# Ranking of the experts moved behind the second expert's weight splits, the fixing of the ranked places' words moved into the second expert, and the first transposes made due later

## The chip, the cores and the metric

The kernel runs on one core of a Trainium2 chip, with everything it needs in the device's memory. The metric is the time of one execution on the device in microseconds, the median of several runs. The core has five engines with a queue each: TensorE (PE; its weight loads are listed as PEld), VectorE (DVE), ScalarE (ACT), GpSimd (POOL) and SyncE (SP). Each issues its instructions strictly in its queue's order, so one that waits holds up all that stand behind it. SyncE and GpSimd also issue most of the transfers between device memory and on-chip memory; 16 DMA engines carry them out.

## The reference

One decoder layer: a mixing part and a routed mixture of experts. The part that the change touches is the routing: each token takes the best of four groups, and the two best of its four experts.

```python
def hier_moe(x, w_rg, b_rg, w_re, b_re, w_gate, w_up, w_down):
    ...
    g_sel = jnp.argmax(g_logits, axis=-1)
    ...
    top_p, top_i = lax.top_k(e_prob, TOP_K_IN_GROUP)
    top_p = top_p / jnp.sum(top_p, axis=-1, keepdims=True)
    weights = p_g * top_p
    expert_id = g_sel[:, None] * EXPERTS_PER_GROUP + top_i
    combine = jnp.sum(jax.nn.one_hot(expert_id, N_EXPERTS, dtype=f32) * weights[..., None], axis=1)
    y = jnp.zeros(xf.shape, f32)
    for e in range(N_EXPERTS):
        h = jax.nn.silu(xt @ w_gate[e]) * (xt @ w_up[e])
        y = y + combine[:, e:e + 1] * (h @ w_down[e]).astype(f32)
    return y.reshape(B, L, D).astype(x.dtype)
```

There are 2048 tokens of width 1024 and 16 experts with a hidden width of 256. Ahead of this stand a projection, a pooling mixer, a gated linear attention and an output projection; behind it a final norm.

## The kernel before

The kernel has two large stages. The dense one runs over 16 tiles of 128 tokens: projections and attention first, then, tile by tile, the output projection (`out_proj`, three parts into the banks sp, o and ds) and the routing (`route_pick`, `route_rest`). For each tile, `route_rest` counts with small matmuls how many tokens each expert has so far, works out each token's slot, and writes a record of 32 bytes through an indirect transfer into the table in device memory. The second stage runs over the 16 experts, each with a fixed number of slots (up to 320, in row parts j of 128, 128 and 64). An expert's rows are gathered by the token numbers of its records (`gather`, `first_rows`), transposed on TensorE into the banks tp and zg (`transposes`, line 955), scaled and split by ScalarE (line 109, high part) and VectorE (line 110, low part), and multiplied by the expert's weights. All large products are made of three matmuls: high by high, low by high, high by low.

The weights come in chunks of 128 x 1024 numbers (512 KB), in the order of `stream`: four gate chunks and two down chunks for each expert. SyncE issues the loads (`load_chunks`, line 765) into five buffers (three called raw, two called wr); `split_chunk` splits each into a high part on ScalarE (line 113) and a low part on VectorE (line 114), which frees the buffer for a later chunk. The first ten chunks (both gates of the first two experts and the first one's down weights) belong to fixed experts. All later ones go by rank: the 14 other experts are worked on in the order of their token counts, so that the larger ones get the longer slots.

`rank_experts` finds that order on VectorE out of the final counts, and writes `place` (an expert's place) and `expert_at` (the expert at a place). SyncE reads `expert_at` place by place (`expert`, line 749) to address the loads: `load_places` (line 1115) loads the table words of the experts at each place into `tab`, and then `load_chunks` loads their weights. Each record also names the token's other expert, and `fix_words` (lines 1125 to 1131) works out from `place` which of the two is worked on second, and sets the words that the rows' stores and adding loads go by.

Two experts begin early: the rows that the first 13 tiles sent to the experts 0 and 1 are gathered while the last tiles are still routed (row parts 0 and 2), and `gate_rows` multiplies them ahead of the main loop; the rest (part 1) follows from `first_rows`. The first of these transposes were written with `added[0]`, so that they stand behind the last tile's first addition of the output projection. In the loop `between(i)` places work between the matmuls of an expert: transposes of the next expert, splits of coming chunks, the fixing of words.

A scheduler places each instruction in its engine's queue by priority and by the times that it assumes. Two helpers bind it: `must_follow` adds a wait, and `queued_after` only fixes the order within a queue.

## Time and profile before

| | before |
|---|---|
| median of 3 runs | 1103.26 us (1103.2 to 1103.97) |
| profiled execution | 1105.13 us, its span in the trace 1103.4 us |
| TensorE busy | 1048.4 us (95% of the span) |
| VectorE busy | 776.6 us (70%) |
| ScalarE busy | 562.8 us (51%) |
| GpSimd busy | 310.5 us (28%) |

Times in the trace are counted from the span's start. The dense stage ends at about 695 us, the early rows of the two fixed experts run from there to about 724 us, and the loop over the experts begins at about 733 us. A busy engine in these views is one that has an instruction under way; matmuls overlap, and the distance from one start to the next is what a matmul costs. In brackets behind a row stands how long the engine was idle before it and which instruction ended that by the profile; where the engine that is named had long been done, it was another, often a transfer.

### The profile page before, as it was taken

The numbers are of one execution on the slowest core, as the hardware profiler recorded it, in microseconds if no ns is written. First come the engines' busy times: TensorE is split into PE (matmuls) and PEld (weight loads), VectorE is DVE, ScalarE is ACT, GpSimd is POOL, SyncE is SP. The second block draws the span as 40 slices with busy tenths as digits, with TensorE's granted clock in tenths as the row PEclk, the third lists the DMA queues.
The fourth block names the chain that finished last, engine by engine and source line by source line (L and its number), as shares of the span: only waits on it lengthen the run. The fifth ranks groups of instructions, "written<-read, shape, count | busy, mean of one in ns | idle before, by whom it ended". The sixth has DMA issues, their size and how long they took to land. (4 is left out here: it accounts for less than half of the span.)

```text
span 1103.4 us, 19138 instructions
## 1 busy us (share of the span) xinstructions
PE 1048.4 (95%) x6614; PEld 940.3 (85%) x6614; DVE 776.6 (70%) x2674; ACT 562.8 (51%) x1192; POOL 310.5 (28%) x272
## 2 busy tenths in 40 slices
PE   6999999999999999999999999989999999998982
PEld 5888888888888889999999999668998989887961
DVE  6476666654555775887777788767777788887863
ACT  7544444434443552333333333557767777677731
POOL 2000000000000000110111013144777788876540
PEclk9999999999999999999999999999999999999996
DMA  8422232211112342444343345389888989899841
GB/s 289 162 67 77 93 112 93 68 49 58 52 66 84 115 158 101 163 135 137 124 148 133 114 145 194 113 230 303 210 246 228 260 248 239 232 281 330 219 152 61
DMA packets 63831, 173.43 MB, mean 157 GB/s; under 512 B 20532, under 2 KB 20837, under 8 KB 63728
## 3 DMA queue, kind: packets, MB, share of 16 engines
q1 hardware_dynamic: 36272, 105.72, 28.6%
q0 software_dynamic: 24864, 57.87, 19.9%
q10 hardware_dynamic: 2592, 8.55, 2.2%
q8 instruction: 54, 0.88, 0.3%
q14 instruction: 49, 0.40, 0.1%
HBM read 142.43 MB, written 56.43 MB: 180 GB/s over the span
## 5 line engine op out<-in xcount | busy, mean ns | idle before, releaser
L443 POOL DMA_DIRECT2D y_dram<-y x16 | 8.7, 541 | 390.6 <-DVE y L441 390.6
L689 POOL DMA_INDIRECT table<-rec,ix x32 | 32.8, 1026 | 190.3 <-DVE tmp L709 92.8
L933 POOL DMA_INDIRECT oe<-xr,tab x38 | 66.7, 1756 | 63.3 <-ACT xr L1061 46.2
L323 PE MATMUL mm<-wb,XL 128*128 128x512 f32 (+1 forms) x240 | 83.6, 349 | 0.0
L324 PE MATMUL mm<-wb,XH 128*128 128x512 f32 (+1 forms) x240 | 82.9, 345 | 0.0
L322 PE MATMUL mm<-wb,XH 128*128 128x512 f32 (+1 forms) x240 | 82.7, 344 | 0.0
L933 POOL DMA_INDIRECT xr<-oe,tab x37 | 73.3, 1981 | 17.6 <-issue 9.8
L525 PE MATMUL mm<-XL,ws 128*128 128x256 f32 (+1 forms) x256 | 73.1, 286 | 0.2 <-DVE XL L114 0.2
L524 PE MATMUL mm<-XH,ws 128*128 128x256 f32 (+1 forms) x256 | 73.1, 286 | 0.0
L526 PE MATMUL mm<-XH,ws 128*128 128x256 f32 (+1 forms) x256 | 72.3, 282 | 0.0
L113 ACT ACTIVATE XH<-xt 128x1024 fp32r<-128x1024 f32 x32 | 33.9, 1059 | 52.9 <-PE mm L526 32.8
L933 POOL DMA_INDIRECT out_dram<-xr,tab x37 | 51.4, 1388 | 22.1 <-DVE sr_y L62 9.3
L114 DVE TENSOR_TENSOR wb<-raw,wb 128x1024 fp32r<-128x1024 f32 x39 | 47.5, 1220 | 7.9 <-ACT wb L113 7.9
L985 PE MATMUL mm<-xl,ws 128*128 128x256 f32 (+2 forms) x168 | 51.3, 305 | 0.0
L984 PE MATMUL mm<-xh,ws 128*128 128x256 f32 (+2 forms) x168 | 51.0, 303 | 0.0
L986 PE MATMUL mm<-xh,ws 128*128 128x256 f32 (+2 forms) x168 | 50.9, 303 | 0.0
L322 PE MATMUL mm<-ws,XH 128*128 128x512 f32 x112 | 47.5, 424 | 2.0 <-ACT XH L113 2.0
L322 PEld LDWEIGHTS mm<-wb,XH 128*128 128x128 f32 x240 | 45.3, 189 | 4.6
L324 PEld LDWEIGHTS mm<-wb,XH 128*128 128x128 f32 x240 | 45.2, 188 | 4.7
L323 PEld LDWEIGHTS mm<-wb,XL 128*128 128x128 f32 x240 | 45.3, 189 | 4.3
L525 PEld LDWEIGHTS mm<-XL,ws 128*128 128x128 f32 x256 | 48.2, 188 | 0.7 <-DVE XL L114 0.4
L526 PEld LDWEIGHTS mm<-XH,ws 128*128 128x128 f32 x256 | 48.5, 189 | 0.3 <-issue 0.2
(663 smaller groups left out, 3842.5 us busy)
## 6 DMA issues: line engine op xcount, KB each, us to landing
raw<-in_wgu_e_dram SPq DMA_DIRECT2D x42, 512.0 KB, 5.7
xt<-in_xT_dram SPq DMA_DIRECT2D x32, 512.0 KB, 3.6
xn<-in_xn_dram SPq DMA_DIRECT2D x32, 512.0 KB, 3.5
wr<-in_wgu_e_dram SPq DMA_DIRECT2D x22, 512.0 KB, 6.2
raw<-in_wd_e_dram SPq DMA_DIRECT2D x20, 512.0 KB, 6.2
hn_dram<-xn ACTq DMA_DIRECT2D x16, 512.0 KB, 3.4
oe<-xn POOLq DMA_DIRECT2D x16, 512.0 KB, 4.2
wr<-in_wd_e_dram SPq DMA_DIRECT2D x12, 512.0 KB, 6.0
```

The source lines that it names most:

```text
L113: return (nc.scalar.activation(hi, src, AF.Copy), (eng or V).tensor_tensor(lo, src, hi.bitcast(F32), op=OP.subtract))
L114: (eng or V).tensor_tensor(lo, src, hi.bitcast(F32), op=OP.subtract))
L322: nc.tensor.matmul(q, xh[:, k, :], wh[:, c0:c1_], start=(k == 0), stop=False)
L323: nc.tensor.matmul(q, xl[:, k, :], wh[:, c0:c1_], start=False, stop=False)
L324: nc.tensor.matmul(q, xh[:, k, :], wl[:, c0:c1_], start=False, stop=(k == KB - 1))
L524: nc.tensor.matmul(ps[:, b], WS[k][0][:, c], XH[:, k, o:], start=(k == 0), stop=False)
L525: nc.tensor.matmul(ps[:, b], WS[k][0][:, c], XL[:, k, o:], start=False, stop=False)
L526: nc.tensor.matmul(ps[:, b], WS[k][1][:, c], XH[:, k, o:], start=False, stop=(k == KB - 1))
L933: return nc.gpsimd.indirect_dma_start(out=out_, out_offset=off if scatter else None, in_=in_, in_offset=None if scatter else off, bounds_c ...
L984: nc.tensor.matmul(p[:, c0:c1_], wh, xh, start=(k == 0), stop=False)
L985: nc.tensor.matmul(p[:, c0:c1_], wh, xl, start=False, stop=False)
L986: nc.tensor.matmul(p[:, c0:c1_], wl, xh, start=False, stop=(k == KB - 1))
```

## The change

Three things move. `rank_experts` no longer runs right behind the routing of the last tile, in the pool of work tiles of the dense stage, but inside the experts' stage, put in VectorE's queue behind the low part of the second expert's last gate chunk (`last_low`). It works in a tile `sq` that `fix_words` and others use as well, and the counts are kept in `place` itself. The two calls of `fix_words` for the ranked places, made in the loop of the second expert, are put in the queue behind the low part of the third expert's transposes that are written just ahead of them (`low[0]`). And the first transposes follow `added[1]` instead of `added[0]`.

```diff
@@ -172,8 +172,8 @@
     late1, late2, late3 = by_expert("late1", 1.0e9, 0.0), by_expert("late2", 0.0, 0.0), by_expert("late3", 0.0, 0.0)
     late_step2 = by_expert("late_step2", 16384.0, -16.0 - 6144.0)
     late0 = iota("late0", 16, 1, base=127 * 48 + 32, pool=sl)
-    counts = sl.tile([128, 16], F32, name="counts")
     place = per.tile([128, 16], F32, name="place")
+    counts = place
     expert_at = per.tile([128, 16], I32, name="expert_at")
     desc4 = iota("desc4", 4, -1, base=4, pool=sl)
     tok_all = iota("tok_all", NT, 128, pm=1)
@@ -711,25 +711,6 @@
         V.tensor_copy(sv[:, 6:7], r)
         return last
 
-    def rank_experts():
-
-        n = NE - FIXED
-        key = wk.tile([128, 16], F32, name="v16")
-        V.scalar_tensor_tensor(key, counts, 16.0, iota16, op0=OP.mult, op1=OP.subtract)
-        sq = wk.tile([128, 512], F32, name="sq", bufs=1)
-        g = sq[:, :n * n].rearrange("p (a b) -> p a b", a=n)
-        inner = lambda x: x[:, None, FIXED:].to_broadcast([128, n, n])
-        outer = lambda x: x[:, FIXED:, None].to_broadcast([128, n, n])
-        V.tensor_tensor(g, inner(key), outer(key), op=OP.is_gt)
-        V.tensor_copy(place[:, :FIXED], iota16[:, :FIXED])
-        V.tensor_reduce(place[:, FIXED:], g, axis=AX.X, op=OP.add)
-        V.tensor_scalar(place[:, FIXED:], place[:, FIXED:], float(FIXED), None, op0=OP.add)
-        V.tensor_tensor(g, inner(place), outer(iota16), op=OP.is_equal)
-        V.tensor_tensor(g, g, inner(iota16), op=OP.mult)
-        at = wk.tile([128, 16], F32, name="t1")
-        V.tensor_reduce(at[:, FIXED:], g, axis=AX.X, op=OP.add)
-        V.tensor_copy(expert_at[:, FIXED:], at[:, FIXED:])
-
 
     DW = [[WB[4 + f][h][:, :1024] for h in range(2)] for f in range(2)]
     stream = [("g", e, k) for e in range(2) for k in range(4)] + [("d", 0, f) for f in range(2)]
@@ -868,7 +849,6 @@
             route_rest(t - 1)
         route_pick(t)
     routed = route_rest(NT)
-    rank_experts()
     c1.close()
 
     rank = per.tile([128, NT], F32, name="rank")
@@ -920,7 +900,7 @@
               + [(xh1[:, k, :], xl1[:, k, :]) for k in range(2)]]
         HB = me.tile([128, 2, 2 * CAP], F32R, name="HB")
         tab_e = me.tile([128, 2, 2, 8], I32, name="tab_e")
-        hidden_done = [None]
+        hidden_done, low = [None], [None]
...
@@ -958,7 +938,7 @@
                     must_follow(t_, [after])
             c0, c1_ = min(cols[j] for j in js), max(cols[j] + rows[j] for j in js)
             xh, xl = XE[e % 2][k]
-            split_scaled(xh[:, c0:c1_], xl[:, c0:c1_], p[:, c0:c1_], nf[:, k:k + 1])
+            low[0] = split_scaled(xh[:, c0:c1_], xl[:, c0:c1_], p[:, c0:c1_], nf[:, k:k + 1])[1]
 
         def split_hidden(hb, h, c0, c1_):
 
@@ -1114,7 +1094,7 @@
         def load_places(lo, hi, which):
             must_follow(nc.sync.dma_start(by_place[:, :, lo:hi], table_by[:, :, which]), table_ops)
 
-        def fix_words(lo, hi, at):
+        def fix_words(lo, hi, at, after=None):
 
             n = hi - lo
             w = tabf.rearrange("p (j e) w -> p j e w", e=NE)[:, :, lo:hi]
@@ -1122,13 +1102,32 @@
             eq = sq[:, :3 * n * NE].rearrange("p (j e x) -> p j e x", j=3, e=n)
             second = sq[:, 384:384 + 3 * n].rearrange("p (j e) -> p j e", j=3)
             full = [128, 3, n, NE]
-            V.tensor_tensor(eq, w[:, :, :, 5:6].to_broadcast(full), iota16[:, None, None, :].to_broadcast(full), op=OP.is_equal)
+            o_ = V.tensor_tensor(eq, w[:, :, :, 5:6].to_broadcast(full), iota16[:, None, None, :].to_broadcast(full), op=OP.is_equal)
+            if after:
+                queued_after(o_, after)
             V.tensor_tensor(eq, eq, at[:, None, None, :].to_broadcast(full), op=OP.mult)
             V.tensor_reduce(second, eq, axis=AX.X, op=OP.add)
             V.tensor_tensor(second, second, iota16[:, None, lo:hi].to_broadcast([128, 3, n]), op=OP.is_lt)
             V.scalar_tensor_tensor(by_place[:, :, lo:hi, 2], second, -OOB, w[:, :, :, 6], op0=OP.mult, op1=OP.add)
             V.tensor_scalar(second, second, OOB, -OOB, op0=OP.mult, op1=OP.add)
             V.tensor_tensor(by_place[:, :, lo:hi, 1], second, w[:, :, :, 6], op=OP.add)
+
+        def rank_experts(after):
+
+            n = NE - FIXED
+            sq = mk.tile([128, D // 2], F32, name="sq")
+            g, key, at = sq[:, :n * n].rearrange("p (a b) -> p a b", a=n), sq[:, 200:216], sq[:, 216:232]
+            queued_after(V.scalar_tensor_tensor(key, counts, 16.0, iota16, op0=OP.mult, op1=OP.subtract), after)
+            inner = lambda x: x[:, None, FIXED:].to_broadcast([128, n, n])
+            outer = lambda x: x[:, FIXED:, None].to_broadcast([128, n, n])
+            V.tensor_tensor(g, inner(key), outer(key), op=OP.is_gt)
+            V.tensor_copy(place[:, :FIXED], iota16[:, :FIXED])
+            V.tensor_reduce(place[:, FIXED:], g, axis=AX.X, op=OP.add)
+            V.tensor_scalar(place[:, FIXED:], place[:, FIXED:], float(FIXED), None, op0=OP.add)
+            V.tensor_tensor(g, inner(place), outer(iota16), op=OP.is_equal)
+            V.tensor_tensor(g, g, inner(iota16), op=OP.mult)
+            V.tensor_reduce(at[:, FIXED:], g, axis=AX.X, op=OP.add)
+            V.tensor_copy(expert_at[:, FIXED:], at[:, FIXED:])
 
         table_rows = table.rearrange("(p n) w -> p n w", n=48)
         s_ = nc.gpsimd.dma_start(tab_e, table_rows.rearrange("p (j e) w -> p j e w", e=NE)[:, 0:2, 0:2])
@@ -1143,12 +1142,14 @@
             XG[e][1] = row_tile()
         with tc.high_priority():
             for k in range(KB):
-                transposes(0, k, (0, 2), added[0])
+                transposes(0, k, (0, 2), added[1])
         early = [gate_rows(0, 0, "mm"), gate_rows(0, 2, "mm", lambda k: k < 6 or transposes(1, k - 6, (0, 2)))]
         must_follow(picked[0], [gate_ops[6]])
         for k in range(4):
-            must_follow(split_chunk()[1], [routed])
+            last_low = split_chunk()[1]
+            must_follow(last_low, [routed])
             load_chunks(min(8 + k, 10))
+        rank_experts(last_low)
         for k in range(2, KB):
             transposes(1, k, (0, 2))
         load_places(0, FIXED, slice(0, FIXED))
@@ -1182,7 +1183,7 @@
                     for k in range(i, i + 2):
                         transposes(e + 1, k, None if e else (1,))
                 if e == 1 and i in (2, 6):
-                    fix_words(*((2, 9) if i == 2 else (9, 16)), place)
+                    fix_words(*((2, 9) if i == 2 else (9, 16)), place, low[0])
                 if e == 0:
                     if i == 0:
                         for op in load_chunks(10 + WRB, mk):
```

What the order of the queues makes of it, at three places. In the new kernel the lines of the helpers behind `rank_experts` have other numbers: the transposes are line 935, the fixing 1105 to 1113, the ranking 1120 to 1130; lines up to 711 keep theirs. Numbers behind an underscore tell buffers apart: wb_86 to wb_101 are the high and low halves of the second weight buffer (wb_86, wb_88, wb_90, wb_92 are the high parts of the second expert's gate chunks, wb_87 and so on the low ones; wb_94 to wb_97 are the down chunks; wb_98 to wb_101 hold rows of the second expert; in the dense stage all of them hold the output projection's weights), ws are the gate chunks of the first and third expert, and xh and xl those experts' transposed rows.

VectorE, the end of the ranking, before:

```order
L727 TENSOR_TENSOR sq<-place,iota_114 128x196
L709 SCALAR_TENSOR_TENSOR tmp,sv_all<-E,lev 128x16
L110 SCALAR_TENSOR_TENSOR wb_99<-zg,vecs,wb_98 128x192
L709 SCALAR_TENSOR_TENSOR tmp,sv_all<-E,lev 128x16
L728 TENSOR_TENSOR sq<-sq,iota_114 128x196
L114 TENSOR_TENSOR wb_87<-raw,wb_86 128x1024
L730 TENSOR_REDUCE t_8623<-sq 128x14
L114 TENSOR_TENSOR wb_89<-raw,wb_88 128x1024
L731 CAST expert_at<-t_8623 128x14
L114 TENSOR_TENSOR wb_91<-raw,wb_90 128x1024
```

and now:

```order
L114 TENSOR_TENSOR wb_97<-raw,wb_96 128x1024
L1126 TENSOR_SCALAR place<-place 128x14
L114 TENSOR_TENSOR HB<-zg,HB 128x2x128
L1127 TENSOR_TENSOR sq<-place,iota_114 128x196
L993 TENSOR_TENSOR h<-mm,h 64x256
L1128 TENSOR_TENSOR sq<-sq,iota_114 128x196
L1129 TENSOR_REDUCE sq<-sq 128x14
L114 TENSOR_TENSOR HB<-tp,HB 128x2x64
L1130 CAST expert_at<-sq 128x14
L110 SCALAR_TENSOR_TENSOR xl_8627<-zg,vecs,xh_8626 128x128
```

Before, the cast that writes `expert_at` stands between the low parts of the second and third gate chunk; now it stands behind the low parts of the first expert's down chunks (wb_95, wb_97) and behind the splits of the first expert's early hidden tiles (HB from zg and from tp).

VectorE, the first fixing instruction of the ranked places (line 1125, now 1105), before:

```order
L114 TENSOR_TENSOR HB<-tp,HB 128x2x64
L110 SCALAR_TENSOR_TENSOR xl_8640<-zg,vecs,xh_8639 128x128
L110 SCALAR_TENSOR_TENSOR xl_8640<-tp,vecs,xh_8639 128x128
L1125 TENSOR_TENSOR sq<-tab,iota_114 128x336
L110 SCALAR_TENSOR_TENSOR xl_8640<-zg,vecs,xh_8639 128x128
L1126 TENSOR_TENSOR sq<-sq,place 128x336
```

and now:

```order
L110 SCALAR_TENSOR_TENSOR xl_8627<-zg,vecs,xh_8626 128x320
L110 SCALAR_TENSOR_TENSOR xl_8627<-tp,vecs,xh_8626 128x320
L114 TENSOR_TENSOR ws_79<-raw,ws_78 128x1024
L110 SCALAR_TENSOR_TENSOR xl_8627<-zg,vecs,xh_8626 128x320
L1105 TENSOR_TENSOR sq<-tab,iota_114 128x336
L114 TENSOR_TENSOR wb_95<-wr,wb_94 128x1024
L1108 TENSOR_TENSOR sq<-sq,place 128x336
```

Before, it stands among the low parts of the first expert's late rows (128 columns); now it stands behind the low part of the third expert's first gate chunk (ws_79), among the low parts of the third expert's rows (320 columns).

TensorE, the first transposes, before:

```order
L572 MATMUL o<-wb_98,yh 128x348
L955 MATMUL tp<-ident,xs_8645 128x128
L955 MATMUL tp<-ident,xg 128x128
L955 MATMUL zg<-ident,xs_8645 128x128
L955 MATMUL zg<-ident,xg 128x128
L573 MATMUL o<-wb_98,yL 128x348
```

and now:

```order
L572 MATMUL ds<-wb_96,yh 128x348
L573 MATMUL ds<-wb_96,yL 128x348
L935 MATMUL tp<-ident,xs_8632 128x128
L935 MATMUL tp<-ident,xg 128x128
L935 MATMUL zg<-ident,xs_8632 128x128
L935 MATMUL zg<-ident,xg 128x128
L574 MATMUL ds<-wb_97,yh 128x348
```

Before, they stand in the second part of the last tile's output projection (bank o, behind its seventh matmul); now they stand in the third part (bank ds, behind its fifth matmul). The last of their eight rounds now ends behind the third part.

## Rows read from the trace of the kernel before

**Rows 1.** The page, first part: busy time of an engine, its share of the span, its instructions.

```profile
PE 1048.4 (95%) x6614; PEld 940.3 (85%) x6614; DVE 776.6 (70%) x2674; ACT 562.8 (51%) x1192; POOL 310.5 (28%) x272
```

**Rows 2.** Waits of TensorE, longest first in total: line that waited, line that it waited for, us in total, times, longest us. The first four are from the stretch 660 to 820 us, the last from 755 us to the end.

```profile
PE zg L955 <- DVE xl L110: 2.8, 1, 2.8
PE tp L955 <- DVE m L597: 1.5, 1, 1.5
PE zg L955 <- DVE wb L110: 1.2, 1, 1.2
PE sp L1006 <- DVE wb L114: 1.1, 1, 1.1
...
PE tp L955 <- ACT xr L1061: 7.1, 5, 3.0
```

**Rows 3.** TensorE in order of time, 684 to 762 us: start, duration, line, what it writes and reads, sizes, and in brackets the idle time before it.

```profile
685.07 0.33 PE L574 MATMUL o<-wb,yh 128*128 128x348 f32 x1
685.24 0.32 PE L572 MATMUL o<-wb,yh 128*128 128x348 f32 x1
687.04 0.30 PE L955 MATMUL tp<-ident,xs 128*128 128x128 f32 x1 [1.49 <-DVE m L597]
687.18 0.27 PE L955 MATMUL tp<-ident,xg 128*128 128x128 f32 x1
...
711.34 0.50 PE L1006 MATMUL sp<-wb,wb 128*128 128x512 f32 x1 [1.06 <-DVE wb L114]
...
712.37 0.63 PE L1004 MATMUL sp<-wb,wb 128*128 128x512 f32 x1
...
723.41 0.39 PE L1006 MATMUL o<-wb,xh 128*64 128x512 f32 x1
...
724.33 0.28 PE L955 MATMUL zg<-ident,xg 128*128 128x128 f32 x1
...
731.09 0.33 PE L955 MATMUL zg<-ident,xg 128*128 128x128 f32 x1 [2.77 <-DVE xl L110]
...
755.76 0.31 PE L986 MATMUL mm<-xh,ws 128*128 128x320 f32 x1
```

**Rows 4.** ScalarE in order of time: the high parts of the first and of the last gate chunk of the third expert.

```profile
742.78 1.06 ACT L113 ACTIVATE ws<-raw 128x1024 fp32r<-128x1024 f32 x1 [0.36 <-DVE HB L114]
...
751.93 1.07 ACT L113 ACTIVATE ws<-raw 128x1024 fp32r<-128x1024 f32 x1 [0.67 <-DMA raw<-in_wgu_e_dram]
```

**Rows 5.** VectorE in order of time, 706 to 755 us.

```profile
706.55 0.17 DVE L649 TENSOR_TENSOR counts<-m,counts 128x16 f32<-128x16 f32 x1
...
709.01 0.35 DVE L727 TENSOR_TENSOR sq<-place,iota 128x196 f32<-128x196 f32 x1
709.28 0.17 DVE L709 SCALAR_TENSOR_TENSOR tmp<-E,lev 128x16 f32<-128x16 f32 x1
...
709.37 0.41 DVE L110 SCALAR_TENSOR_TENSOR wb<-zg,vecs,wb 128x192 fp32r<-128x192 f32 x1
...
710.06 1.22 DVE L114 TENSOR_TENSOR wb<-raw,wb 128x1024 fp32r<-128x1024 f32 x1
...
712.60 0.17 DVE L731 CAST expert_at<-t 128x14 int32<-128x14 f32 x1
...
725.45 0.29 DVE L114 TENSOR_TENSOR HB<-tp,HB 128x128 fp32r<-128x128 f32 x1
...
730.27 0.51 DVE L1125 TENSOR_TENSOR sq<-tab,iota 128x336 f32<-128x336 f32 x1 [3.11 <-DMA tab<-table]
...
754.37 1.22 DVE L114 TENSOR_TENSOR ws<-raw,ws 128x1024 fp32r<-128x1024 f32 x1
```

**Rows 6.** SyncE: the reads of expert_at (durations in ns, least, median, most; first and last start in us), then its transfers in order of time (start, time from the first to the last issue's end, count).

```profile
L749 SPq TENSOR_LOAD <-expert_at x14: 262/270/727, 716.1 to 731.1; - x14
715.36 16.76 SPq L1115 DMA_DIRECT2D tab<-table  x15
...
733.02 0.35 SPq L765 DMA_DIRECT2D raw<-in_wgu_e_dram  x1
```

**Rows 7.** Transfers, by the stretch in which they were issued: line's tiles, queue, count, size, us from issue to landing. The first was issued between 733.0 and 733.1, the second between 745.0 and 745.5, the third between 680.2 and 681.0 us. Last, the part of GpSimd's queue in the stretch 740 to 744 us: packets, MB, share of the 16 engines' time.

```profile
raw<-in_wgu_e_dram SPq DMA_DIRECT2D x1, 512.0 KB, 5.4
...
raw<-in_wgu_e_dram SPq DMA_DIRECT2D x1, 512.0 KB, 6.8
...
xg<-hn_dram,tab_e POOLq DMA_INDIRECT x1, 4.3
...
q0 software_dynamic: 159, 0.59, 62.5%
```

**Rows 8.** Stretches: length, then busy us (instructions) of PE, PEld, DVE, ACT and POOL, TensorE's granted clock (1.00 is 2.4 GHz), mean busy share of the DMA engines, GB/s.

```profile
710.00:720.00 10.00, 8.94 (x37) 6.08 (x37) 8.40 (x16) 4.81 (x8) 2.68 (x3) 0.83 0.54 164
...
730.00:740.00 10.00, 8.91 (x43) 6.29 (x44) 8.54 (x28) 5.79 (x15) 4.15 (x3) 1.00 0.79 211
...
748.00:750.00 2.00, 2.00 (x14) 1.59 (x12) 2.00 (x3) 1.90 (x4) 0.00 (x0) 1.00 1.03 416
```

**Rows 9.** GpSimd in order of time: the last write of records into the table, the gather of the first expert's late rows, and a gather for the fourth expert.

```profile
710.53 1.61 POOL L689 DMA_INDIRECT table<-rec,ix  x1 [0.31 <-issue]
...
719.15 1.12 POOL L933 DMA_INDIRECT xg<-hn_dram,tab  x1 [7.01 <-DMA tab<-table]
...
740.15 1.04 POOL L933 DMA_INDIRECT xg<-hn_dram,tab  x1 [1.68 <-PE tp L955]
```

## The prediction

> **What bounds the kernel now.** I first read the shares of the engines: TensorE is busy for 95% of the span [rows 1], so only its few idle stretches and what they hide can matter. The second view is the list of its waits between 660 and 820 us, where the change works [rows 2]: four stalls of 2.8, 1.5, 1.2 and 1.1 us, 6.6 us in all. The third view puts them in order of time [rows 3]: 1.49 us ahead of 687.04 (the first transposes), the 1.2 and 1.1 us close together ahead of 711.34 (the rows of the second expert, behind the routing of the last token tile), 2.77 us ahead of 731.09. The reader should then see what else is late at the end of this stretch. At 751.93 ScalarE has waited 0.67 us for a weight load, and splits the last weights of the third expert [rows 4]; VectorE finishes their low part at 754.37 + 1.22 = 755.59 [rows 5], and TensorE takes it at 755.76 [rows 3]. So at 755 us the kernel is bound by weights that arrive just in time, not by TensorE's earlier stalls. After that its largest waits are a few for gathered rows, 7.1 us over 350 us [rows 2], so I take a shift at 755.76 to reach the end one for one.
>
> **Where those weights come from.** SyncE's queue issues in order: the table words of the first two experts at 715.36, then 14 times "read expert_at, load that expert's table words" (reads from 716.1 to 731.1), then the final norm's weights, then at 733.02 the first 512 KB chunk of the third expert [rows 6]. That chunk takes 5.4 us (to 738.4), and the sixth, issued just behind 745.0, lands 6.8 us later, at 751.9 [rows 7], which is the wait in rows 4. From 733.02 to 751.9 are 18.9 us.
>
> **The change, part by part.**
>
> First transposes due later. They now stand behind 22 more matmuls of the output projection, at 0.17 us each (685.07 to 685.24 [rows 3]): 685.4 + 3.7 = 689.1. The rows that they waited for were there at 687.04, so the 1.49 us go. Against it, the second pair of transposes needs a bank that VectorE frees only behind the routing instructions that the order puts ahead of it; following its queue I find it free some 0.4 us late. Net -1.1 us (bounds -1.5 and 0).
>
> Ranking out of the last routing. Between the counts at 706.55 and the first low split at 710.06 VectorE spends 3.5 us [rows 5]. Six ranking instructions lie in it: four of 196 elements at 0.27 us (709.01 to 709.28) and two small ones at 0.09 (709.28 to 709.37), so 1.26 us. The order puts two low parts of 192 columns there instead (0.41 each) and takes two small accumulations out (0.18): 3.5 - 1.26 + 0.82 - 0.18 = 2.9 us, 0.6 us less. TensorE's 711.34 becomes 711.34 - 1.1 - 0.6 = 709.6, or 710.0 if the low parts wait for their transposes, with four more transposes already done (0.14 us each, 687.04 to 687.18 [rows 3]): a lead of about 1.8 us. In before TensorE fell to its lower clock right after this stall: the matmul at 712.37 takes 0.63 us against 0.50 at 711.34 and 0.39 at 723.41 [rows 3], and the granted clock of 710 to 720 is 0.83 [rows 8], which is 0.17 of 10 us or 1.7 us lost. With a shorter stall it may stay at 2.4 GHz, 1.7 us more lead, or not.
>
> This lead does not last. The routing's own last cast comes only 0.3 us earlier (most of the ranking leaves ahead of it, three low parts enter). So the second table write (710.53 [rows 9]), the table words (715.36) and the gather of the first expert's late rows (719.15 [rows 9]) move by 0.3 us. That gather takes 4.3 us at the least (the quickest of its kind [rows 7]), 718.9 + 4.3 = 723.2, and TensorE needs its rows for the transpose that stands at 724.33 [rows 3]. It comes there at about 721 and waits about 2 us: the lead is 1.1 us at most.
>
> Fixing words in the second expert. At 730.27 VectorE has waited 3.11 us for the table words of the ranked places, with the low parts of the transposes queued behind it [rows 5], and TensorE stalls 2.77 us for that [rows 3]. In the new order these words come behind the third expert's low parts, some 15 us later, when they have long landed. The stall goes, and TensorE's lead grows to about 3.9 us. The fourteen fixing instructions, 0.5 us for the widest (730.27), then lie between the weight splits; one of the widest is ahead of the last split and costs 0.3 us there, where the split waits for ScalarE in part.
>
> Ranking behind the low parts. Here is the price. The cast that writes expert_at stood at 712.60 [rows 5], 3.5 us ahead of the first read at 716.1 [rows 6], so it cost nothing. In the new order it stands behind the split of the second early hidden tile (HB from tp). In before that split is at 725.45 [rows 5]; it needs TensorE's transposes of h, which stand one matmul ahead of the end of the second expert's 48 matmuls. Behind 710.0 these are 43 matmuls of 0.23 us (723.41 to 724.33 is four of them [rows 3]) and six transposes of 0.14, 10.7 us: 720.7. ScalarE's and VectorE's halves, the matmul and the cast are four short steps, 1.2 us: **the cast is at about 722.0** (721 if all goes well, 723.5 if the clock falls as in before). SyncE's queue stops there, with everything behind it. Its 14 reads and loads take as long as before, so the first chunk goes from 733.02 to 722.05 + (733.02 - 716.1) = 739.0, 6.0 us later.
>
> What of this hides. TensorE's lead hides nothing, since it ends in waiting for the weights themselves. Two things shorten the chain behind the first chunk. In before ScalarE came to it only at 742.78 [rows 4], 4.4 us after landing; now it waits for it, and the sixth chunk, whose buffer the first one's split frees, is asked for 7.8 us after the first instead of 12, which no longer binds. And the gathers of later experts, which shared the DMA engines with the chunks (0.59 MB on GpSimd's queue in 740 to 744, 62.5% of the engines' time [rows 7]), are now mostly ahead of 739. Bounds: with the same company the sixth chunk lands at 739.0 + 18.9 = 757.9, +6.0 us; with none, the five chunks behind the first follow it at 0.524 MB by the best rate near here, 416 GB/s [rows 8], 1.3 us each: 739.0 + 5.4 + 6.3 = 750.7, which is -1.2 us. I take the two gathers of 512 KB out of the company that fell behind the first chunk (the later one at 740.15 [rows 9]), 1.05 MB by 416 GB/s, 2.5 us: 755.4, +3.5 us. It is nearer the upper end because GpSimd still stores the first expert's rows in that stretch.
>
> The Trainium skill ("DMA: Bandwidth & Descriptors", Queues, rings and completion order) says that each DMA engine takes turns packet by packet between the queues that have work. By it the chunks have about half of the engines while GpSimd's queue has work and all of them otherwise, which would give the same two ends and leaves open only how long the company lasts; the 62.5% of rows 7 agree with a share of that kind.
>
> **The sum.** Sixth chunk +3.5, one fixing instruction +0.3: the low part at 755.59 and the matmul behind it come 3.8 us later. The leads of 1.1 and 2.8 us are spent in waiting for it. The profiled execution took 1105.13 us with a span of 1103.4; the median of the runs is 1103.26, and I add the shift to that: **1107.0 us**.
>
> **The rivals.**
> 1. The chunks catch up: GpSimd's queue is nearly empty after 739, chunks follow each other at 1.3 to 1.9 us, and the sixth lands before 753.8. Then the shift is -1 to +2 us, 1102 to 1105, which a measurement can't tell from no change (0.2%, 2.2 us). For it speaks that TensorE's lead moves the stores and gathers forward; against it, that the DMA engines were busy throughout in 748 to 750 (share 1.03 [rows 8]), 15 us behind the first chunk.
> 2. Faster: the lead of 3.9 us reaches the experts, 1099.4 us. It decides from the point at which the sixth chunk lands by 748, that is, if the cast comes by 714 or so, or the chunks are not held behind it. For it speaks the size of the removed stalls, most of 6.6 us. The order of the queues speaks against it.
> 3. A second price: TensorE now waits in pieces between 747 and 759 for each chunk, and the clock falls behind them, as after 711.34. That cost 1.7 us there; on top of the forecast it gives 1108.7, and with the clock's fall also ahead of the cast (+1.5) 1110.2. In this trace the 2.77 us ahead of 731.09 did not bring a fall (granted clock 1.00 in 730 to 740 [rows 8]), so I keep it as the smaller case. The Trainium skill ("TensorE: Matmul & The Clock Gate", HAM oscillation) tells of a kernel that pays the fall again at every wait for a load; by it 1108.7 would be the likelier of the two, and of the two stalls of this trace one agrees.
>
> That the change doesn't do what it says I leave out: the order shows it.
>
> **How the numbers follow.** Forecast 0.50, rival 1 0.27, rival 2 0.08, rival 3 0.15. The forecast and rival 3 are slower by over 0.2%, less a little of the forecast's low end (0.02) that counts as same; rival 1 is the same. Faster 0.08, same 0.29, slower 0.63. The range runs from rival 1's low end, 1102, to 1110.5, which takes in the bound with the same company (+6.3, 1109.6); what is left out is rival 2 and the worst of rival 3, about 0.12.
>
> **What would show it.** No stall at 687; a shorter one ahead of the second expert's low part; a new wait of about 2 us for the gathered rows at about 721 to 723; none of 2.8 us behind the fixing. The cast of expert_at at 722, the first read right behind it, the first chunk's issue at 738 to 741. ScalarE waiting for several raw chunks between 743 and 756, and TensorE's matmul on the third expert's last low part at 757 to 762 against 755.76. I am wrong if that matmul comes earlier than 755, if expert_at is read ahead of 716, or if time is lost or won behind 764 us, where I expect nothing but the shift.

## The result, and the profile after

The changed kernel takes 1110.83 us (median of 8 runs, 1106.85 to 1113.16), the kernel before 1103.32 in the same set (1101.06 to 1104.99): a ratio of 1.0059, 95% interval 1.0042 to 1.0076, slower by 4.6 to 8.4 us. The forecast was 1107.0, the range 1102.0 to 1110.5; the median lies 0.3 us above the range, the sign is right. The profiled execution took 1112.83 us, its span is 1110.7.

First a correction that the comparison needs. The last tile's first matmul on bank o, where nothing of the change has acted yet, starts at 684.29 us before and at 687.02 after, 2.73 us later. In later profiles of both kernels (e5, e6) it starts at 683.94 and 684.27, and in the other ten between 683.65 and 685.71, so I take it for a difference between executions. Below, "net" means less 2.73.

TensorE's waits in the stretch 660 to 830 us, of after (line waited, line waited for, us in total, times, longest); they answer to [rows 2]:

```profile
PE zg L935 <- DVE xl L110: 3.6, 1, 3.6
PE zg L935 <- DMA xg<-hn_dram,tab: 2.6, 1, 2.6
PE sp L986 <- DVE wb L114: 1.2, 1, 1.2
...
PE mm L966 <- DVE ws L114: 0.5, 1, 0.5
```

The same waits in TensorE's order of time, of after:

```profile
692.03 0.33 PE L935 MATMUL tp<-ident,xs 128*128 128x128 f32 x1 [0.24 <-DVE xn L577]
...
712.43 0.50 PE L986 MATMUL sp<-wb,wb 128*128 128x512 f32 x1 [1.25 <-DVE wb L114]
...
726.47 0.45 PE L935 MATMUL zg<-ident,xg 128*128 128x128 f32 x1 [2.63 <-DMA xg<-hn_dram,tab]
...
754.25 0.48 PE L935 MATMUL zg<-ident,xs 128*128 128x128 f32 x1 [3.56 <-DVE xl L110]
...
761.31 0.41 PE L966 MATMUL mm<-xh,ws 128*128 128x320 f32 x1 [0.46 <-DVE ws L114]
...
763.25 0.50 PE L1025 MATMUL sp<-wb,HB 128*128 128x512 f32 x1 [0.47 <-ACT HB L113]
...
763.89 0.41 PE L966 MATMUL mm<-xh,ws 128*128 128x320 f32 x1
```

Against [rows 3]: the 1.49 us ahead of the first transposes are 0.24, the 1.2 and 1.1 us behind the routing are one wait of 1.25, the 2.77 us of the fixing are gone. In their place stand 2.63 us for gathered rows and 3.56 us ahead of the third expert's transposes. The second is a wait for weights, as ScalarE's order of time shows, of after (against [rows 4]):

```profile
751.42 1.06 ACT L113 ACTIVATE ws<-raw 128x1024 fp32r<-128x1024 f32 x1 [4.61 <-DMA raw<-in_wgu_e_dram]
752.39 0.51 ACT L109 ACTIVATE xh<-zg,vecs 128x320 fp32r<-128x320 f32 x1
...
755.07 1.06 ACT L113 ACTIVATE ws<-raw 128x1024 fp32r<-128x1024 f32 x1 [0.81 <-DMA raw<-in_wgu_e_dram]
...
758.82 1.06 ACT L113 ACTIVATE ws<-raw 128x1024 fp32r<-128x1024 f32 x1 [0.16 <-DMA raw<-in_wgu_e_dram]
```

ScalarE stands 4.61 us for the first chunk; the high part of the transposes (752.39) is queued behind it, so VectorE's low part and then TensorE's bank zg are late. Where the chunk was, VectorE and SyncE show, of after (against [rows 5, 6]):

```profile
724.39 0.16 DVE L1130 CAST expert_at<-sq 128x14 int32<-128x14 f32 x1
```

```profile
729.49 11.02 SPq L1095 DMA_DIRECT2D tab<-table  x10
740.62 0.56 SPq L1161 DMA_DIRECT2D fw<-in_fnw_dram  x1
741.43 0.47 SPq L746 DMA_DIRECT2D raw<-in_wgu_e_dram  x1
...
748.81 5.30 SPq L746 DMA_DIRECT2D raw<-in_wgu_e_dram  x2
```

(The first row is ten of the fifteen loads of table words.) The cast is at 724.39, net 721.7 (712.60 before); the first chunk is issued at 741.43, net 738.7 (733.02 before). What the waits don't show is the clock. Stretches of after, then of before (length, busy us of PE, PEld, DVE, ACT, POOL, granted clock, DMA share, GB/s), which answer to [rows 8]:

```profile
710.00:720.00 10.00, 8.69 (x41) 5.89 (x40) 8.44 (x32) 4.17 (x8) 2.83 (x2) 1.00 0.51 161
720.00:726.00 6.00, 3.84 (x18) 1.98 (x16) 4.17 (x11) 1.50 (x4) 3.00 (x2) 1.00 0.36 96
726.00:736.00 10.00, 9.53 (x41) 7.15 (x41) 5.67 (x18) 5.68 (x14) 4.57 (x5) 0.83 0.69 176
736.00:750.00 14.00, 14.00 (x72) 10.61 (x71) 5.18 (x14) 5.87 (x14) 6.07 (x5) 1.00 1.07 277
750.00:754.00 4.00, 0.70 (x4) 0.22 (x2) 1.49 (x2) 2.58 (x4) 0.00 (x0) 0.92 1.00 350
754.00:762.00 8.00, 7.10 (x28) 6.06 (x29) 8.00 (x16) 5.74 (x8) 1.09 (x1) 0.61 0.83 283
762.00:772.00 10.00, 9.39 (x43) 6.46 (x42) 6.80 (x16) 5.80 (x11) 5.88 (x5) 1.00 0.91 266
```

```profile
728.00:738.00 10.00, 7.23 (x35) 4.88 (x34) 6.77 (x20) 4.72 (x13) 3.68 (x3) 1.00 0.83 198
738.00:746.00 8.00, 8.00 (x42) 5.99 (x41) 6.05 (x16) 6.11 (x12) 1.52 (x2) 1.00 1.04 333
746.00:756.00 10.00, 9.86 (x58) 8.13 (x57) 8.77 (x14) 7.71 (x14) 4.47 (x4) 1.00 1.01 358
```

After the change the clock holds at 2.4 GHz behind 712, where it fell before (0.83 in 710 to 720 [rows 8]), but it falls to 1.2 GHz behind each of the two new waits: 0.83 over 10 us is 1.7 us of clock lost, 0.92 over 4 and 0.61 over 8 are 3.4. Before, the stretch up to 756 has no second fall.

**One account for all runs.** A is the last tile's first matmul on bank o, B the third expert's first matmul of its down projection (bank sp, operand HB): 684.29 and 777.60 before, 687.02 and 786.22 after. "Waits" adds up TensorE's idle times in brackets from A to B; "clock" adds, over stretches of 5 us, their length times (1 - granted clock). "Counts" is VectorE's addition that gives the final counts. All in us of one profiled execution; the ratio is that of the timed runs to the kernel before in the same set. The three sets of experiments (e1 to e4, e5 to e8, e9 to e12) ran on three chips, on which the kernel before took 1108.91, 1107.06 and 1108.73; the expectations in us were written for its 1103, so they are read against before in the same set.

| run | ratio, 95% interval | A to counts | counts to cast | counts to first chunk | waits | clock | A to B |
|---|---|---|---|---|---|---|---|
| before | | 22.26 | 6.05 | 26.47 | 6.54 | 1.70 | 93.31 |
| after | 1.0059 (1.0042 to 1.0076) | 21.10 | 16.27 | 33.31 | 8.79 | 5.15 | 99.20 |
| e5 before again | 1.0007 (0.9984 to 1.0030) | 23.88 | 6.05 | 27.42 | 8.44 | 5.15 | 97.27 |
| e6 after again | 1.0078 (1.0051 to 1.0105) | 25.80 | 16.27 | 35.78 | 13.69 | 8.55 | 106.61 |
| e2 ranking alone | 1.0048 (1.0026 to 1.0070) | 24.33 | 16.26 | 35.16 | 14.51 | 3.40 | 103.84 |
| e3 all but the ranking | 1.0016 (0.9998 to 1.0033) | 27.12 | 6.04 | 27.86 | 10.51 | 8.55 | 102.59 |
| e10 fixing alone | 1.0025 (1.0007 to 1.0042) | 23.91 | 6.05 | 28.47 | 9.98 | 5.15 | 99.79 |
| e11 transposes alone | 1.0004 (0.9984 to 1.0024) | 25.48 | 6.05 | 27.60 | 8.98 | 5.10 | 98.42 |
| e7 cast alone | 1.0092 (1.0057 to 1.0128) | 24.94 | 19.02 | 39.64 | 13.35 | 8.60 | 106.97 |
| e9 chunks alone | 1.0041 (1.0019 to 1.0064) | 25.74 | 6.04 | 34.66 | 12.22 | 6.85 | 104.09 |
| e1 ranking earlier | 1.0042 (1.0023 to 1.0061) | 26.14 | 12.40 | 30.20 | 12.48 | 5.10 | 102.68 |
| e8 ranking earlier still | 1.0079 (1.0052 to 1.0105) | 25.85 | 10.27 | 26.90 | 12.31 | 6.85 | 103.77 |
| e4 after, other queue order | 1.0110 (1.0082 to 1.0137) | 27.11 | 16.23 | 20.53 | 15.49 | 10.25 | 108.98 |
| e12 e10, other queue order | 1.0075 (1.0051 to 1.0098) | 23.97 | 6.05 | 20.50 | 14.85 | 6.85 | 102.96 |

From before to after, A to B grows by 5.89 us: 2.25 of waits and 3.45 of clock make 5.70 of it. From e5 to e6 it grows by 9.34: 5.25 and 3.40 make 8.65. This tells how TensorE spent the time, not what set it: a fall of the clock in a stretch where TensorE would otherwise wait for weights need not add to it (the part on the prediction comes back to this). Ahead of A lie the 2.73 (e6: 0.33); behind B the changed kernel is 1.3 us quicker (324.48 against 325.80 to the span's end), in e6 2.3.

The table has one execution of each kernel, and the ratios are better evidence than its last columns: behind B the fourteen profiles take between 321.31 us (e1) and 327.28 (e8), and the profiled execution can lie off the median, in e3 by 3.7 us (1114.76 against 1111.08). So e3 has a long A to B and a ratio near 1.

### The profile page after: what moved, and what is told of

Its sections match the earlier page's. It is cut to its first block, busy times and chain, and to the rows that moved or that the text cites. A ratio compares the mean times of both kernels' runs of the same rounds, so it can differ in the third digit from the quotient of the medians.

```text
span 1110.7 us, 19135 instructions
## 1 busy us (share of the span) xinstructions
PE 1052.0 (95%) x6614; PEld 941.7 (85%) x6614; DVE 776.2 (70%) x2674; ACT 563.3 (51%) x1192; POOL 316.1 (28%) x272
## 3 DMA queue, kind: packets, MB, share of 16 engines
q10 hardware_dynamic: 2592, 8.55, 2.1%
```

## The experiments

**The parts of the change, one at a time (e2, e3, e10, e11).** e2 is the kernel before with the new ranking; e3 is the changed kernel without it:

```diff
-        rank_experts(last_low)                                # e3
+    rank_experts()                                            # behind the last route_rest, as before
```

> The kernel before with the ranking alone moved behind the fourth low part; first transposes and fixing of words as before. Theory: the cast is at 722 to 725, the first chunk at 739 to 742, the matmul on ws31 3 to 6 us behind that of before, and the time 1107 to 1111 us, about that of the full change. Rival (the loss comes from the later first transposes or from the later fixing of words): 1101 to 1104 us.

> The changed kernel with the ranking back in the routing of the last tile; the first transposes later and the fixing of words behind the low parts stay. Theory: the cast is at 712 to 713, the first chunk at 732 to 734, the stalls of 1.5 and 2.8 us are gone but the lead is spent in waiting for the weights, the matmul on ws31 is within 1.5 us of before, and the time is 1101.5 to 1104.5 us. Rival (removed stalls reach the end): 1098 to 1100 us. Rival (the loss comes from these two edits): 1107 us or more.

The ranking alone gives 1.0048, all without it 1.0016 with an interval that takes in 1; the two together are about the change's 1.0059. The cast and the first chunk move with the ranking and with nothing else. So most of the loss is the ranking's, as the theory of e2 says. e3's own forecast holds less well: the two stalls are there in its profile (3.76 us ahead of the first transposes, 3.61 us ahead of the late ones, behind a ScalarE that stands idle for 5.08), and its median is 2.2 us above before, where at most 1.2 was expected.

```diff
-                    fix_words(*((2, 9) if i == 2 else (9, 16)), place)
+                    fix_words(*((2, 9) if i == 2 else (9, 16)), place, low[0])     # e10
```
```diff
-                transposes(0, k, (0, 2), added[0])
+                transposes(0, k, (0, 2), added[1])     # e11
```

> The kernel before with the fixing of the ranked places' words alone moved behind the third expert's low parts; ranking in the routing, first transposes as before. The stall of 2.8 us ahead of the first expert's late transposes goes. Theory (the kernel before is bound at 755 us by weights that arrive just in time): the lead is spent in waiting for them, and the time is within 1.5 us of before. Rival (the removed stall reaches the end): 2 to 3 us under before.

> The kernel before with the first transposes alone due later, behind the second part of the last tile's sum. By the forecast: the wait ahead of the first transposes is gone or under 0.3 us, 1.1 us won there and spent at 755 us, the time within 1 us of before. Rival, from e1, e3, e4, e6 and e8: the sum that they now wait for stands at the end of VectorE's queue behind the routing of the tile before, TensorE waits 3.5 us for it instead of 1.2 and 1.7, the counts come 1 to 2 us later, and the time is 1 to 2.5 us above before.

e10 is not quicker but slower by 0.8 to 4.7 us, which neither theory gave. The stall that it should remove is there all the same, for another reason; TensorE in e10, then in e5 (the kernel before on another chip), and ScalarE in e5:

```profile
731.15 0.48 PE L955 MATMUL zg<-ident,xg 128*128 128x128 f32 x1 [3.57 <-DVE xl L110]
```

```profile
730.55 0.48 PE L955 MATMUL zg<-ident,xg 128*128 128x128 f32 x1 [2.88 <-DVE xl L110]
```

```profile
725.34 0.36 ACT L1012 ACTIVATE h<-mm 64x256 f32<-64x256 f32 x1
729.74 0.37 ACT L109 ACTIVATE xh<-zg,vecs 128x128 fp32r<-128x128 f32 x1 [4.04 <-remote]
```

In these executions ScalarE stands 4 to 5 us ahead of that high part ("remote": released by nothing that the trace names), and the table words have come by then. In the first profile of before ScalarE does not stand there, and the fixing is the stall. So what e10 could win was tested only where the stall has a second cause. A part of why it is slower shows in its trace: TensorE waits for the third expert's last low part, which stands on VectorE behind fixing instructions (TensorE, then VectorE, of e10):

```profile
760.01 0.41 PE L986 MATMUL mm<-xh,ws 128*128 128x320 f32 x1 [0.69 <-DVE ws L114]
```

```profile
757.67 0.50 DVE L1129 TENSOR_REDUCE sq<-sq 128x21 f32<-128x336 f32 x1
758.18 0.55 DVE L110 SCALAR_TENSOR_TENSOR xl<-tp,vecs,xh 128x320 fp32r<-128x320 f32 x1
758.65 0.17 DVE L1130 TENSOR_TENSOR sq<-sq,iota 128x21 f32<-128x21 f32 x1
758.73 1.23 DVE L114 TENSOR_TENSOR ws<-raw,ws 128x1024 fp32r<-128x1024 f32 x1
```

Four of them (lines 1125 and 1128 to 1130) take 1.4 us from one start to the next there, without a pause of VectorE; e5 and e11, which fix the words earlier, have no such wait, and e3 has the same 0.69. The rest stays open.

e11 makes no difference that can be measured, as forecast, but not by the forecast's way. TensorE in order of time and VectorE, of e11:

```profile
693.66 0.33 PE L955 MATMUL tp<-ident,xs 128*128 128x128 f32 x1 [3.24 <-DVE xn L577]
```

```profile
693.10 0.51 DVE L577 TENSOR_TENSOR xn<-o,xn 128x348 f32<-128x348 f32 x1
```

The sum that the transposes now follow stands behind the routing of the tile before on VectorE, which runs late. e1, e3, e4, e6 and e8 have the same wait (3.6 to 3.8 us); only the first profile of after has 0.24. Kernels with the old due time wait 1.2 to 1.7 and then 1.4 to 2.0 us in the same sets (e5, e9, e10, e12), so little is lost or won.

**The mechanism (e6, e7, e9).** e5 and e6 repeat before and after; e7 moves the one cast (until then the ranking's result stands as f32 in the bytes of expert_at), e9 holds only the chunks:

```diff
+            if k == 2:                                        # e7, in early_rest
+                queued_after(cast, hidden_done[0])
```
```diff
-                    if i == 0:                                # e9
+                    if i == 4:
                         for op in load_chunks(10 + WRB, mk):
-                            must_follow(op, first_rows)
+                            must_follow(op, first_rows + [low[0]])
```

> The kernel before, unaltered, for a profile from the same chip as the runs beside it. Both theories: the same time as before within 0.3%. In the profiles of the first four experiments VectorE and ScalarE stood idle in pieces of 1 to 5 us that no other engine or transfer explains (1.3 and 1.1 us ahead of the first transposes in e1, 5.1 us of ScalarE at 733 us in e3). If that belongs to the chip, this profile shows them too, with TensorE's first transposes 2 to 4 us late; if it belongs to the edits, this profile has none, as the first profile of before.

> The changed kernel, unaltered, beside e5. Theory (late cast): 4 to 9 us above before on the same chip; from the last tile's first matmul on bank o to the third expert's first matmul on HB and bank sp 3 to 6 us more than in e5 (76.23 against 71.13 in the first two profiles). Rival (the +7.5 us were half run-to-run, in the dense stage and behind the stretch): 2 to 4 us above before.

> The kernel before with one instruction moved: the ranking stays in the routing, but the cast that writes expert_at (14 numbers, 0.17 us) is queued behind the split of the second early hidden tile, where the changed kernel has it. (The scheduler then also puts the fixing of the ranked places' words later by itself.) Theory (the late cast alone is the price): cast 16 us behind the counts instead of 6, first chunk of the third expert 5 to 9 us later than in e5, and the time 3 to 7 us above before. Rival (the cast costs nothing, the ranking's or the transposes' other effects do): within 1.5 us of before.

> The kernel before with one wait added: the third expert's first chunks are also held until the low part of the sixth of the second expert's late-row transposes (at about 739 us in the first profile of before). The cast of expert_at, the gathers, the ranking, the fixing of words and the first transposes stay as before, and so does the order of VectorE, ScalarE and GpSimd. Theory (the weights' lateness is the price): the first chunk goes from 27 us behind the counts to 32 to 35 (33.3 in the changed kernel), and the time is 3 to 7 us above before. Rival (the late cast costs by another way, by the gathers of the third expert's rows that also stand behind it, and the chunks catch up): within 1.5 us of before.

(The mark named in the expectation of e6 is the second expert's down projection, by which e6 is 7.4 us behind e5 where 3 to 6 were expected; the table uses the third's.) e5 has the unexplained idle pieces, so they don't come from the edits. e6 is 5.6 to 11.6 us above before. Moving one instruction of 0.17 us (e7) costs 0.57 to 1.28%, 6.3 to 14.2 us, more than the 3 to 7 expected; the scheduler moved the fixing too, and the cast came even later than in the changed kernel (19.0 us behind the counts), the first chunk 12.2 us later than in e5. In e9 the cast, the gathers and the order on every engine, but for a few matmuls of TensorE, are as before, and only the chunks are late, by 6 to 7 us (34.66 against 27.60 and 28.47 in e11 and e10); it costs 0.19 to 0.64%, 2.1 to 7.1 us. ScalarE and the stretch behind, of e9:

```profile
750.91 1.06 ACT L113 ACTIVATE ws<-raw 128x1024 fp32r<-128x1024 f32 x1 [2.83 <-DMA raw<-in_wgu_e_dram]
753.49 1.06 ACT L113 ACTIVATE wb<-wr 128x1024 fp32r<-128x1024 f32 x1 [1.51 <-DMA wr<-in_wd_e_dram]
```

```profile
756.00:762.00 6.00, 5.25 (x21) 4.42 (x22) 4.42 (x7) 4.91 (x9) 1.56 (x1) 0.72 0.84 244
```

It is the picture of after: ScalarE waits for the chunks, TensorE's transposes stand 3.52 us behind it, the clock falls. So late chunks alone make a loss of this kind, 0.41% against the 0.59 and 0.78 of the change. Whether the gathers of the third expert's rows, which also stand behind the late cast (21.7 us behind the counts against 15.4), add to it in after and e7 is open.

**The ranking, but earlier (e1, e8).**

```diff
             load_chunks(min(8 + k, 10))
+            if k == 0:
+                cast = rank_experts(last_low)
+            if k == 3:                                        # e8 only
+                queued_after(last_low, cast)
-        rank_experts(last_low)
```

> The changed kernel, with the ranking queued behind the first of the four low parts instead of the fourth; all else as changed. Theory (the late cast of expert_at holds SyncE's queue, and the third expert's weights come late): the cast comes at about 716 to 718 instead of 724.6, the first chunk of the third expert is issued at 733 to 735 instead of 741.4, the matmul on ws31 comes at 755 to 758, and the time is 1103 to 1106 us. Rival (the cast costs nothing in the end; the loss lies in the dense stage, +2.7 us by the two profiles, and behind the stretch, +1.8): 1109 to 1112 us, wherever the cast stands.

> The changed kernel with the ranking queued behind the first of the four low parts and the fourth low part queued behind the cast, so that no wait for the last chunks stands ahead of it. Theory: the cast is 9 to 12 us behind the counts (16.3 in the changed kernel, 12.4 in e1, where two low parts that waited for their chunks stood ahead of it), the first chunk 4 to 6 us earlier than in e6, the time 2.5 to 6 us under e6, within 0.25% of before. Rival (the loss lies elsewhere): within 1.5 us of e6.

Both theories missed; e8's rival holds by its number (1116.98 against e6's 1116.06). In e1 the cast fell behind two low parts that wait for their chunks and was only 4 us earlier. In e8 it was 6 us earlier, the first chunk came as early as in e5 (26.9 against 27.4), and the time did not come back. ScalarE, TensorE and two stretches of e8:

```profile
746.39 1.06 ACT L113 ACTIVATE ws<-raw 128x1024 fp32r<-128x1024 f32 x1 [0.58 <-DVE h L993]
749.88 1.06 ACT L113 ACTIVATE wb<-wr 128x1024 fp32r<-128x1024 f32 x1 [2.43 <-DMA wr<-in_wd_e_dram]
...
752.71 1.06 ACT L113 ACTIVATE ws<-raw 128x1024 fp32r<-128x1024 f32 x1 [1.19 <-DMA raw<-in_wgu_e_dram]
```

```profile
755.54 0.47 PE L935 MATMUL zg<-ident,xs 128*128 128x128 f32 x1 [3.94 <-DVE xl L110]
```

```profile
752.00:756.00 4.00, 0.46 (x2) 0.46 (x3) 2.35 (x4) 3.29 (x5) 1.39 (x1) 0.85 1.03 418
756.00:764.00 8.00, 8.00 (x38) 7.12 (x37) 5.21 (x9) 4.07 (x7) 0.48 (x1) 0.65 0.79 276
```

ScalarE takes the first chunk 35.2 us behind the counts (746.39 - 711.20); in e5 it does so at 39.1. TensorE and ScalarE arrive 4 us earlier, with the lead that the removed stalls give, at weights that are asked for no earlier: the second chunk, issued 27.2 us behind the counts, is waited for until 38.7. The lead becomes a wait of 3.94 us, and the clock falls behind it, at 0.15 x 4 + 0.35 x 8 = 3.4 us. What the last weights wait for is no longer the chunks: ScalarE splits the last one at 758.03, 46.8 us behind the counts (47.2 in e5), but its low part starts only at 764.42 (VectorE, of e8):

```profile
762.88 0.55 DVE L110 SCALAR_TENSOR_TENSOR xl<-zg,vecs,xh 128x320 fp32r<-128x320 f32 x1 [2.62 <-ACT xh L109]
...
764.42 1.22 DVE L114 TENSOR_TENSOR ws<-raw,ws 128x1024 fp32r<-128x1024 f32 x1
```

It stands behind fixing instructions and behind low parts of transposes that TensorE makes late. So the theory's size was wrong: with the first and the last chunk as early as in e5 this order is still slower. That is not all of it, since behind B e8 also takes 4.3 us more than e6, which nothing here explains.

**Another order of SyncE's queue (e4, e12).**

```diff
-        for e in range(FIXED, NE):
-            load_places(e, e + 1, expert(e))
+        load_places(FIXED, FIXED + 1, expert(FIXED))
         first_rows = [...]
+        for op in load_chunks(13, mk):                        # e4; 15 in e12
+            must_follow(op, first_rows)
+        for e in range(FIXED + 1, NE):
+            load_places(e, e + 1, expert(e))
         gather(2)
```

> The changed kernel with the order of SyncE's queue altered: the table words of the third expert, then three chunks of its weights, and only then the other thirteen reads of expert_at with their table words. The cast stays late, at about 724. Theory (the price is that the chunks stand behind fourteen reads that wait for the cast): the first chunk is issued at 726 to 728, the weights are there in time, and the time falls by 3 us or more against the changed kernel, to 1102 to 1107 us. Rival (the late cast costs by another way, or the loss lies elsewhere): within 1.5 us of the changed kernel, 1109 to 1112 us.

> e10 with SyncE's queue in another order: behind the table words of the third expert's place stand five chunks of its weights and two of its down rows, and only then the other thirteen reads of expert_at with their table words. Theory (chunks earlier, with the cast early, let the lead of the removed stall through): the first chunk 19 to 23 us behind the counts instead of 27, no wait for weights at 745 to 760 us, 1.5 to 4 us under before. Rival (as in e4, the thirteen reads and loads then lie beside the chunks' transfers and take longer, and the sixth chunk or the table words come late): 1 us or more above before.

e12 is slower than e10, from which it was made, as its rival says. e4 missed both of its expectations: it is 10.7 us above before, which is more than after by the ratios, though its interval touches that of e6 on another chip. The first chunk came 12.8 us (e4) and 8.0 us (e12) earlier than in the kernel that was altered, the next one that needed a freed buffer far later, behind thirteen reads and loads. SyncE and ScalarE in e12:

```profile
734.04 18.23 SPq L1115 DMA_DIRECT2D tab<-table  x13
...
753.22 0.47 SPq L765 DMA_DIRECT2D raw<-in_wgu_e_dram  x1
```

```profile
760.69 1.06 ACT L113 ACTIVATE ws<-raw 128x1024 fp32r<-128x1024 f32 x1 [10.48 <-DMA raw<-in_wgu_e_dram]
```

The loads took 18.2 us for thirteen beside the chunks (16.8 for fifteen before [rows 6]); the sixth chunk was asked for at 753.2, and ScalarE waited 10.48 us for it. Here the late asking for the last chunks costs more than the early first one gives. No version beat the kernel before.

## Why the prediction was right in sign and short in size

- **First transposes**: -1.1 forecast; A to counts went from 22.26 to 21.10, -1.16. In the repeated pair it is not there (25.80 in e6 against 23.88 in e5), nor in e11, so it may be luck of the first pair.
- **Ranking out of the routing**: the wb matmul forecast at 709.6 to 710.0 came at 712.43, net 709.7; the clock held there.
- **New wait for gathered rows**: about 2 us, ending at 723.2, was forecast; it was 2.63, ending at 726.47, net 723.7. The clock fell behind it (1.7 us lost), which the sum left out.
- **Fixing of words**: its stall is gone in after, as forecast; e10 shows no gain from it where ScalarE stands idle there anyway. What it costs behind was put too low, see below.
- **Cast and chunk**: 722.0 and 739.0 forecast, net 721.7 and 738.7 measured. e7 and e9 show that this lateness alone costs several us.
- **Sixth chunk**: +3.5 us forecast; ScalarE's last gate split went from 751.93 to 758.82, net +4.2, within the bounds. That this is so close is luck, for the way there was another. The first chunk landed 9.9 us after its issue, not 5.4: GpSimd's queue, which was to be mostly done by then, had 39.5% of the DMA engines' time in 741 to 752 us. The sixth was asked for at about 753.8, when VectorE had freed the first one's buffer, 12.4 us behind the first and not 7.8, and then landed in about 5.0 us, not 6.8.
- **One fixing instruction**: +0.3 forecast; eight of the fourteen lie ahead of the last low part. VectorE, of after:

```profile
752.51 1.23 DVE L114 TENSOR_TENSOR ws<-raw,ws 128x1024 fp32r<-128x1024 f32 x1 [5.08 <-ACT ws L113]
...
754.12 0.50 DVE L1105 TENSOR_TENSOR sq<-tab,iota 128x336 f32<-128x336 f32 x1
...
762.20 0.51 DVE L1105 TENSOR_TENSOR sq<-tab,iota 128x336 f32<-128x336 f32 x1
762.61 1.23 DVE L114 TENSOR_TENSOR ws<-raw,ws 128x1024 fp32r<-128x1024 f32 x1
```

From 752.51 to the end of the last low part at 763.84 VectorE does not pause once (8.00 of 8.00 us busy in 754 to 762), so each instruction there pushes back all that follow, and the eight take 2.1 us from one start to the next. The last low part starts 2.7 us behind the end of ScalarE's last split, against 1.4 before.
- **Shift at ws31** (the third expert's last low part): +3.8 forecast. The matmul on it is the one at 763.89, 0.05 us behind the end of the low part; the one at 761.31 takes the low part of the third of the four chunks. So the shift is 763.89 - 755.76 - 2.73 = +5.4. At B it is 5.9.

The mis-sized terms are thus the two of the sum, +3.5 and +0.3: they came out as +4.16 and +1.36, and 1103.26 + 5.5 is 1108.8. The rest of the way to 1110.83 is not in the account of this change: the profiled pair differs by 7.3 us, of which 5.9 lie from A to B, 2.73 ahead of A and -1.3 behind B.

Rival 3 held that TensorE would wait in pieces and the clock fall behind them, priced at 1.7 and 3.2 us on top. The falls came: one was gone and two are new, of 1.7 and 3.4 us. But that they add to the time is not shown. The matmul on the last low part starts as soon as VectorE has written it; had the clock held, TensorE would have waited longer for the same weights. What the falls add in the other runs is open. The forecast with 3.4 us of falls on top would be 1110.4, near the 1110.83, but that is no evidence, since the sum's own terms came out otherwise as well.

Whether a wait is followed by a fall was not to be told from its length alone. The forecast went by one wait of 2.77 us that brought none [rows 8]. Of the waits for gathered rows in the changed order, 2.63 us in after, 2.66 in e8 and 2.54 in e4 came with a fall, 2.75 in e1, 2.51 in e6 and 2.32 in e2 did not; those of 3.56 in after, 4.09 in e1, 3.94 in e8 and 3.52 in e9, ahead of the third expert's transposes, all did. The Trainium skill ("TensorE: Matmul & The Clock Gate", HAM oscillation) tells of a kernel in which the fall is paid again at every wait for a load. These traces agree for the longer waits and differ for the three shorter ones without a fall.

The step "the leads are spent in waiting" was right: after, TensorE waits 3.56 us ahead of the third expert's transposes and again for the low parts. That nothing but the shift happens behind holds nearly: B to the end differs by -1.3 us, in the repeated pair by -2.3. Not settled: the 2.73 us ahead of A, why VectorE and ScalarE stand idle in the later sets, what the gathers add, and most of why e10 is slower.

## What to carry to other kernels

An instruction of 0.17 us can cost 5 us or more if a queue waits on it and what is queued behind ends just in time; ask of each moved instruction which queue stops for it. Where a stage is bound by weights that arrive just in time, the leads won ahead of it ended in waiting (after, e8). Work that is moved beside late weights is not free: when all the chunks come late, the engine that splits them has no pause left, and each instruction put between the splits counts in full. A fall of TensorE's clock is a price of its own only where TensorE, and not the weights, sets the time; ask at the last instruction of the stretch what it waited for. And make sure that a mark is the same instruction in both traces: count the matmuls of its group, for several may look alike.

## What was not expected of the hardware

- The clock's loss from A to B comes in steps: 1.70, 3.40, 5.10 to 5.15, 6.85, 8.55 to 8.60 and 10.25 us in the fourteen profiles, that is whole multiples of about 1.7 us. One fall can hold more than one of them, as the second of after (3.4).
- On three chips VectorE and ScalarE stood idle in pieces of 1 to 5 us that no engine or transfer in the trace explains, in the kernel before too (4.04 us in e5); the first profiles of before and after have none over 1.4 in the same stretch (a wait of 3.67 us of ScalarE at 723.39, of before, ends as TensorE's transposes of h are done). The kernel before took 1107.06 to 1108.91 us on these chips, 1103.32 in the set of after.
